# A hybrid decoder layer: rotary angles computed at the start, row scalings on ScalarE, five PSUM banks for the input projection, gate columns as stationary weights

## The chip, the cores and the metric

The kernel runs on one core of a Trainium2 chip. The metric is the device time of one execution in microseconds (us), taken as the median of several runs. Beside it stands one profiled execution, from which all rows below are read.

## What is computed

One decoder layer over 256 tokens of width 2048, in float32. Two projections of the conditioning vector `c` and of the normalised tokens feed two causal mixers, whose outputs share one output projection; then comes an expert channel mixer (PEER) over 16384 experts.

```python
mod = jax.nn.silu(c) @ w_ada + b_ada                    # 6 x 2048 shifts, scales, gates
h = modulate(rms_norm(x, norm1_g), shift1, scale1)
proj = h @ w_in                                         # 2048 x 6160
gq, gk, gv, gg, ga, mq, mk, mv = jnp.split(proj, offs, axis=-1)
log_a = jax.nn.log_sigmoid(ga @ gla_w_a2 + gla_b_a) / 16    # ga: 16 columns a token
o_gla = gla_attention(...); o_gla = rms_norm(o_gla, gla_norm_g) * silu(gg)
qm, km = partial_rotary(rms_norm(mq, ...), positions), partial_rotary(rms_norm(mk, ...), positions)
o_moba = moba_attention(qm, km, mv)                     # softmax rows p = exp(s - max) / sum
x = x + gate1 * (jnp.concatenate([o_gla, o_moba]) @ w_out)
x = x + gate2 * peer_ffn(modulate(rms_norm(x, norm2_g), shift2, scale2), ...)
```

With 256 tokens there is one MoBA block, so that the attention is causal within it. The rotary part needs the cosine and sine of 16 angles for every token.

## The kernel before

The kernel has a **front** (normalisation, projections, mixers; here up to about 545 us) and, behind it, the PEER part. The change touches the front alone. There, TensorE (PE) computes `w_in` and `w_out` products with operands split into a high and a low float32r half (`mm3`: three matmuls for a product). A block of weights of 128 x 1024 (512 KB) is loaded by SP (`w_load`), ScalarE makes its high half (`split_hi`, L164) and GpSimd (POOL) its low half (`split_lo`, L168), both some three blocks ahead.

The work is a list `items` of **steps**, one weight block each: 96 of the input projection (`project`, 12 matmuls with 512 columns), then 32 of the output projection. A column block of the projection takes two PSUM banks, one for each half of the tokens, and spans one step in steps 0 to 23, two in steps 24 to 71 and four from 72 on. When it is through, `after(tt)` adds the bank to an SBUF tile on VectorE (DVE, L486) or, the first time, copies it on ScalarE (L484); that is issued one step later (`late`). Banks come from three pools: `mm_ps` has three banks, `tp_ps` two, `at_ps` two. The tag `acc` has one.

DVE has a second stream of work: the product of `silu(c)` with `w_ada`, 160 loads of 512 KB in the front (`ada_load`, `ada_op`). An operation multiplies one loaded block into an accumulator (L260, L262, L265; mostly two instructions of 512 columns). How many run in a step is decided when the program is built, by a planned time `clock["PE"]` that `pe` advances with each matmul's columns. Every load that is used up issues the next (SP waits for that buffer, and what stands behind it in SP's queue waits too). DVE runs in program order: sums of banks, ada operations, and the steps of generators (`begins`) that are moved on once a step.

Those generators are what is touched: `small_loads` (from step 2) loads the positions among others, converts them (L400) and forms angles on POOL (L405); `angle_steps` (from step 12) reduces the angles on DVE (L427 to L441), takes the sine (L443) and multiplies the tables `tabs` (L449); `attend` (from step 76) divides the softmax rows on DVE (L551, L552), `normed` (in `gla`) scales rows of the GLA output (L720). `first_h` makes a quarter of the modulated input `h1`; step 24 is the first that needs the second quarter (L189). The 16 gate columns `pga` are computed in four groups, at column block 7, with the tokens as stationary weights and 16 columns moving; `gla` then transposes them.

Of the kernel before, what the change touches and what calls it, by code (L numbers as in the profile page):

```python
# [46 lines left out]
GLA = 90  # L47
# [24 lines left out]
def hybrid_layer(ctx, tc, x, xt, c, pos, w_ada0, w_ada, w_gate, b_cols, n1g, w_in, w_ga, wa2, ba, gla_g, q_g, k_g,  # L72
# [320 lines left out]
    ga = c1.tile([128, 2, 16], F32, name="ga")  # L393

    def small_loads():
        D_ = nc.sync
# [4 lines left out]
        V.tensor_tensor(gahl[:, 1], wga, gahl[:, 0].bitcast(F32), op=OP.subtract)
        D_.dma_start(out=wa2t[0:16], in_=wa2)
        D_.dma_start(out=wa2t[16:17], in_=ba)
        for tt in range(2):
# [10 lines left out]
    cs = c1.tile([128, 2, 2, 16], F32, name="cs")  # L415
    tabs = c1.tile([128, 2, 2, 4, 16], F32, name="tabs")
    freq = c1.tile([128, 16], F32, name="freq")
    fr = np.power(np.float32(500000.0), -np.arange(16, dtype=np.float32) * np.float32(2.0 / 32))
    for i in range(16):
        G.memset(freq[:, i:i + 1], float(fr[i]))  # L420
    posf = c1.tile([128, 2], F32, name="posf")
    ang = c1.tile([128, 2, 2, 16], F32, name="ang")
    kk = c1.tile([128, 2, 2, 16], F32, name="kk")
    magic = 1.5 * 2.0 ** 23

    def reduce_by(a, k, period, bits, n):
        V.tensor_scalar(k, a, 1.0 / period, magic, op0=OP.mult, op1=OP.add)  # L427
        V.tensor_scalar(k, k, magic, None, op0=OP.subtract)
        for p in _pieces(period, bits, n):
            V.scalar_tensor_tensor(a, k, -p, a, op0=OP.mult, op1=OP.add)  # L430

    def angle_steps():
        reduce_by(ang[:, :, 1], kk[:, :, 1], 2 * math.pi * 4096, 7, 4)
        yield
        reduce_by(ang[:, :, 1], kk[:, :, 1], 2 * math.pi, 10, 3)
        yield
        V.tensor_scalar(ang[:, :, 0], ang[:, :, 1], math.pi / 2, None, op0=OP.add)
        yield
        reduce_by(ang[:, :, 0], kk[:, :, 0], 2 * math.pi, 10, 3)
        yield  # L440
        V.tensor_scalar(ang, ang, 3.1415925, -3.1415925, op0=OP.min, op1=OP.max)  # L441
        yield
# [13 lines left out]

    def project(q, n, hf, group, part):

        first, last = (q, hf) == group[0], (q, hf) == group[-1]
        if first:  # L460
            held["ps"] = [mm_ps(), mm_ps()]
# [10 lines left out]
        if n == 7:  # L472
            pga = mm_ps("pga")
            rows = [(q_, k) for q_, hf_ in group for k in range(2 * hf_, 2 * hf_ + 2)]
            for tt in range(2):
                for q_, k in rows:
                    ts, cs_ = slice(128 * tt, 128 * (tt + 1)), slice(16 * (4 * q_ + k), 16 * (4 * q_ + k + 1))
                    mm3(pga[:, 16 * tt:16 * (tt + 1)], h1[q_][:, 0, k, ts], h1[q_][:, 1, k, ts], gahl[:, 0, cs_], gahl[:, 1, cs_],
                        (q_, k) == rows[0], (q_, k) == rows[-1])

        def after(tt):
# [5 lines left out]
            if tt and pga is not None:  # L487
                p3 = pga[:, 0:32].rearrange("p (t r) -> p t r", t=2)
                if q == 0 and hf == 0:
                    V.tensor_copy(ga, p3)  # L490
                else:
                    V.tensor_tensor(ga, ga, p3, op=OP.add)
# [38 lines left out]
    def attend(tt, h0):  # L531
# [20 lines left out]
        V.tensor_tensor(sm, sm, den[:, :, None].to_broadcast([128, nh, 128 * nk]), op=OP.mult)  # L552
# [35 lines left out]
    def gla():  # L588
        pgT = tp_ps("pgT")
        for tt in range(2):  # L590
            P.transpose(pgT[0:16, 128 * tt:128 * (tt + 1)], ga[:, tt], ident)
        yield
        V.tensor_copy(gaT[0:16], pgT[0:16, 0:T])
        yield
# [117 lines left out]
        def normed(tt, oo, sq):  # L712
# [7 lines left out]
            V.tensor_tensor(oo, oo, r[:, :, None].to_broadcast([128, 8, 128]), op=OP.mult)  # L720
# [95 lines left out]
    for step, it in enumerate(items):  # L816
# [592 lines left out]
```

## Time and profile before

| | us |
|---|---|
| median of three runs (2169.94 to 2176.66) | 2176.55 |
| the profiled execution, its own time | 2170.98 |
| its span, first to last instruction | 2169.2 |
| PE busy in the span | 2058.6 (95%) |
| DVE busy | 1626.8 (75%) |
| POOL / ACT busy | 937.5 / 891.2 |
| moved by DMA | 484.10 MB, 223 GB/s |

The page gives shares over the whole span; the stages have different limits, so the reading starts from the front's stretches. A row of the timeline shows the start, the duration from first to last instruction of a group, and in brackets the idle time before it with the instruction that ended it. "PEclk" is the granted clock of PE: 1.00 is 2.4 GHz and 0.50 is 1.2 GHz.

### The profile page before, as it was taken

The page shows a single profiled execution, that of the slowest core. Times are in us where ns is not written, and L with a number is a line of the kernel's source. Part 1 is how long each engine was busy: PE and PEld are TensorE (multiplying, and loading weights), DVE is VectorE, ACT ScalarE, POOL GpSimd, SP SyncE. Part 2 cuts the span into 40 slices and gives each one's busy share as a digit, 9 for nine tenths or more (in the row PEclk, how much of TensorE's full clock was granted, in tenths as well). Part 3 has the DMA queues.
Part 4 walks back from the last instruction along what each step waited for, and adds up shares of the span by engine and source line. Part 5 has one row for each costly group of instructions (what it writes and reads, how often), then busy time and mean ns, then how long its engine had stood idle before and what let it go on. Part 6 is the DMA issues. An engine that isn't in the chain of part 4 may idle for free.

```text
span 2169.2 us, 33001 instructions
## 1 busy us (share of the span) xinstructions
PE 2058.6 (95%) x12470; PEld 1795.2 (83%) x12470; DVE 1626.8 (75%) x2784; ACT 891.2 (41%) x1184; POOL 937.5 (43%) x551
## 2 busy tenths in 40 slices
PE   4899989989898798999999999999999999999998
PEld 3677777889898798888888888888888888888886
DVE  6787888985785687878788776777677676777687
ACT  5433454533444233434334434444344444444443
POOL 3677855555578777666666666520000000000000
PEclk9899989999899899999999999999999999999999
DMA  8788978878764566667676777776666666666674
GB/s 300 284 298 310 349 271 310 301 270 316 217 214 150 127 166 155 178 183 192 181 211 182 190 203 191 210 207 215 217 223 219 211 224 210 226 220 220 200 238 142
DMA packets 201569, 484.10 MB, mean 223 GB/s; under 512 B 54833, under 2 KB 88113, under 8 KB 200770
## 3 DMA queue, kind: packets, MB, share of 16 engines
q1 hardware_dynamic: 163250, 476.59, 65.1%
q0 software_dynamic: 36864, 0.15, 4.7%
q10 hardware_dynamic: 1296, 5.24, 0.7%
q8 instruction: 99, 1.62, 0.3%
q14 instruction: 60, 0.49, 0.1%
HBM read 469.05 MB, written 12.85 MB: 222 GB/s over the span
## 4 chain that ended last, share of the span: by engine, by line
PE 72%; DVE 5%; POOL 2%; issue 1%; DMA 1%; ACT 0%; SPq 0%; DVEq 0%; ACTq 0%; POOLq 0%
PE out L134 24%; PE A L134 17%; PE pa L134 15%; PE rot L134 8%; PE mm L134 2%; PE pq L134 2%; PE pg L1179 1%; POOL hl L168 1%; DVE acc L262 1%; POOL eq L999 1%; PE po L134 1%; DMA raw<-in_w_ada_dram 0%; DVE hl L168 0%; PE ada_ps L134 0%; DMA spread<-zeros 0%
## 5 line engine op out<-in xcount | busy, mean ns | idle before, releaser
L164 ACT ACTIVATE hl<-raw 128x1024 fp32r<-128x1024 f32 x672 | 675.4, 1051 | 431.7 <-PE mm L134 148.3
L168 DVE TENSOR_TENSOR hl<-raw,hl 128x1024 fp32r<-128x1024 f32 x506 | 607.5, 1228 | 128.1 <-ACT hl L164 127.0
L1193 POOL DMA_INDIRECT spread<-worth,place x256 | 470.9, 1839 | 245.2 <-DMA spread<-worth,place 205.8
L134 PE MATMUL out<-hl,wt 128*128 128x512 f32 x2304 | 570.4, 390 | 0.0
L134 PEld LDWEIGHTS out<-hl,wt 128*128 128x128 f32 x2304 | 430.8, 188 | 89.8
L168 POOL TENSOR_TENSOR hl<-raw,hl 128x1024 fp32r<-128x1024 f32 x166 | 401.3, 2422 | 208.8 <-ACT hl L164 194.3
L134 PE MATMUL A<-hT,hl 128*128 128x512 f32 (+1 forms) x2144 | 389.3, 340 | 0.0
L134 PE MATMUL pa<-hT,hl 128*128 128x256 f32 x2928 | 372.3, 287 | 16.2 <-POOL hl L168 16.2
L134 PEld LDWEIGHTS A<-hT,hl 128*128 128x128 f32 x2144 | 333.1, 188 | 51.9
L134 PEld LDWEIGHTS pa<-hT,hl 128*128 128x128 f32 x2928 | 360.8, 194 | 17.6 <-POOL hl L168 17.4
L1337 POOL TENSOR_TENSOR fin<-fin,back 128x512 f32<-128x512 f32 x4 | 5.1, 1276 | 726.1 <-DVE fin L1336 726.1
L134 PE MATMUL mm<-hl,hT 128*128 128x512 f32 x1152 | 289.8, 409 | 29.0 <-DVE mq L486 4.0
L134 PEld LDWEIGHTS mm<-hl,hT 128*128 128x128 f32 x1152 | 222.2, 196 | 83.1 <-DVE mk L486 4.9
L262 DVE SCALAR_TENSOR_TENSOR acc<-raw,sc,acc 128x512 f32<-128x512 f32 (+1 forms) x308 | 217.1, 705 | 35.2 <-DMA raw<-in_w_ada_dram 27.7
L1329 DVE TENSOR_TENSOR accs<-accs,rot 128x512 f32<-128x512 f32 x252 | 171.7, 681 | 81.3 <-PE rot L134 81.1
L134 PE MATMUL rot<-hl,wt 128*128 128x512 f32 x768 | 219.2, 394 | 2.2 <-DVE mod L160 1.4
L134 PEld LDWEIGHTS rot<-hl,wt 128*128 128x128 f32 x768 | 141.0, 188 | 31.3 <-issue 3.5
L1050 ACT ACTIVATE gel<-both 128x256 f32<-128x256 f32 x67 | 28.1, 419 | 320.1 <-DVE both L1049 308.9
L1048 DVE COPY both<-A 128x256 f32<-128x256 f32 x67 | 28.4, 424 | 132.4 <-PE A L134 132.4
L1233 ACT ACTIVATE wt<-wf 128x256 fp32r<-128x256 f32 x128 | 53.5, 418 | 170.1 <-DVE wf L1229 119.3
L134 PE MATMUL pq<-hT,hl 128*128 128x256 f32 x768 | 100.1, 291 | 7.8 <-DVE hT L876 4.1
L1026 ACT ACTIVATE gel<-pa 128x256 f32<-128x256 f32 x61 | 23.4, 383 | 198.9 <-PE pa L134 180.0
(250 smaller groups left out, 1506.4 us busy)
## 6 DMA issues: line engine op xcount, KB each, us to landing
raw<-in_u_dram SPq DMA_DIRECT2D x256, 512.0 KB
raw<-in_v_dram SPq DMA_DIRECT2D x256, 512.0 KB
raw<-in_w_ada_dram SPq DMA_DIRECT2D x160, 512.0 KB
raw<-in_w_in_dram SPq DMA_DIRECT2D x96, 512.0 KB
raw<-in_w_out_dram SPq DMA_DIRECT2D x32, 512.0 KB
raw<-in_w_q_dram SPq DMA_DIRECT2D x32, 512.0 KB
raw<-in_w_gate_dram SPq DMA_DIRECT2D x32, 512.0 KB
spread<-zeros SPq DMA_DIRECT2D x26, 320.0 KB
```

The lines of the kernel that those rows point to most:

```text
L134: P.matmul(out, lhs, rhs, **kw)
L164: S.activation(t[:, 0], r, AF.Copy)
L168: eng.tensor_tensor(t[:, 1], r, t[:, 0].bitcast(F32), op=OP.subtract)
L262: V.scalar_tensor_tensor(acc, part, sc[:, kb:kb + 1], acc, op0=OP.mult, op1=OP.add)
L999: G.tensor_tensor(eq, eq, indf[:, tt, cc, :, None, :].to_broadcast([128, 2, 16, 16]), op=OP.mult)
L1026: S.activation(gel_of(j), pa[:, 0:T], AF.Gelu)
L1048: V.tensor_copy(both, pa[:, 0:T])
L1050: S.activation(gel_of(j), both, AF.Gelu)
L1179: P.matmul(pg[:, t].rearrange("p s j -> p (s j)"), p1[t // 8][:, t % 8 // 2, :, t % 2], p2[:, t // 2, :, :, t % 2].rearrange("p s j -> p ( ...
L1193: G.indirect_dma_start(flat, bass.IndirectOffsetOnAxis(ap=place[:, tt, k:k + 1], axis=0), worth[:, tt, k:k + 1], None, compute_op=OP.add)
L1233: S.activation(wt[:, 0], wf, AF.Copy)
L1329: V.tensor_tensor(acc[n, tt], acc[n, tt], ps, op=OP.add)
```

## The change

It has six parts.

- The load of the positions is issued second in SP's queue, and the rotary angles are computed right behind DVE's first constants, before its first ada operation; the products of positions and frequencies move from POOL to DVE. The generator that is left (`table_steps`) takes the sine and multiplies `tabs` on POOL instead of DVE.
- The division of the softmax rows, and the scaling of the GLA rows by their inverse norm, become one ScalarE instruction for each head (16 and 16 in all) with the factor as its scale.
- `in_ps` gives the input projection banks in turn from `mm_ps` (three) and `at_ps` (two), until step 73; then from `mm_ps` alone, as before.
- The gate columns `pga` are computed with the 16 columns of weights standing and 256 tokens moving, 48 matmuls in place of 96; the result is already transposed, so that two transposes and a copy in `gla` go, and DVE's copy or sum has 16 x 256 elements in place of 128 x 32.
- No more than two ada operations run from the planner in one step.
- The GLA generator starts at step 92 in place of 90 (it has two stages less).

```diff
+    nc.sync.dma_start(out=posi, in_=pos)
...
+    V.tensor_copy(posf, posi)
+    for tt in range(2):
+        V.tensor_scalar(ang[:, tt, 1], freq, posf[:, tt:tt + 1], None, op0=OP.mult)
+    reduce_by(ang[:, :, 1], kk[:, :, 1], 2 * math.pi * 4096, 7, 4)
+    reduce_by(ang[:, :, 1], kk[:, :, 1], 2 * math.pi, 10, 3)
+    V.tensor_scalar(ang[:, :, 0], ang[:, :, 1], math.pi / 2, None, op0=OP.add)
+    reduce_by(ang[:, :, 0], kk[:, :, 0], 2 * math.pi, 10, 3)
+    V.tensor_scalar(ang, ang, 3.1415925, -3.1415925, op0=OP.min, op1=OP.max)
...
-                V.tensor_tensor(tabs[:, i, :, j], cs[:, :, c_], qkg[:, i:i + 1, 16 * g_:16 * (g_ + 1)].to_broadcast([128, 2, 16]), op=OP.mult)
+                G.tensor_tensor(tabs[:, i, :, j], cs[:, :, c_], qkg[:, i:i + 1, 16 * g_:16 * (g_ + 1)].to_broadcast([128, 2, 16]), op=OP.mult)
...
+    def in_ps(name="mm"):
+
+        held["turn"] = held.get("turn", -1) + 1
+        return (mm_ps if held["turn"] % 5 < 3 or ada["step"] >= ATTENDS[0] - 3 else at_ps)(name)
...
-            held["ps"] = [mm_ps(), mm_ps()]
+            held["ps"] = [in_ps(), in_ps()]
...
-            for tt in range(2):
-                for q_, k in rows:
-                    ts, cs_ = slice(128 * tt, 128 * (tt + 1)), slice(16 * (4 * q_ + k), 16 * (4 * q_ + k + 1))
-                    mm3(pga[:, 16 * tt:16 * (tt + 1)], h1[q_][:, 0, k, ts], h1[q_][:, 1, k, ts], gahl[:, 0, cs_], gahl[:, 1, cs_],
-                        (q_, k) == rows[0], (q_, k) == rows[-1])
+            for q_, k in rows:
+                cs_ = slice(16 * (4 * q_ + k), 16 * (4 * q_ + k + 1))
+                mm3(pga[0:16, 0:T], gahl[:, 0, cs_], gahl[:, 1, cs_], h1[q_][:, 0, k], h1[q_][:, 1, k],
+                    (q_, k) == rows[0], (q_, k) == rows[-1])
...
-        V.tensor_tensor(sm, sm, den[:, :, None].to_broadcast([128, nh, 128 * nk]), op=OP.mult)
+        for h in range(nh):
+            S.activation(sm[:, h], sm[:, h], AF.Copy, scale=den[:, h:h + 1])
...
-            V.tensor_tensor(oo, oo, r[:, :, None].to_broadcast([128, 8, 128]), op=OP.mult)
+            for h in range(8):
+                S.activation(oo[:, h], oo[:, h], AF.Copy, scale=r[:, h:h + 1])
...
-        while coming and 1.456 * (len(raws) + ada["loaded"]) + LEAD < clock["PE"] + (SLOPE * step + MORE * max(0, step - 58)) / 100:
+        most = ada["done"] + 2
+        while coming and ada["done"] < most and 1.456 * (len(raws) + ada["loaded"]) + LEAD < clock["PE"] + (SLOPE * step + MORE * max(0, step - 58)) / 100:
```

Three places show how instructions move. On DVE, at the start of the program (constants, then the ada accumulator `acc`), the order before was:

```order
L325 MEMSET chunk_of 128x2
L326 MEMSET chunk_of 64x1
L327 MEMSET chunk_of 64x1
L260 TENSOR_SCALAR acc<-raw,sc 128x256
L262 SCALAR_TENSOR_TENSOR acc<-raw,sc,acc 128x256 x7
```

and now it is, from the same memset on (the first nine instructions of the angles are left out here):

```order
L343 TENSOR_SCALAR kk<-ang 128x2x16
L344 TENSOR_SCALAR kk<-kk 128x2x16
L346 SCALAR_TENSOR_TENSOR ang<-kk,ang 128x2x16 x3
L353 TENSOR_SCALAR ang<-ang 128x2x16
L343 TENSOR_SCALAR kk<-ang 128x2x16
L344 TENSOR_SCALAR kk<-kk 128x2x16
L346 SCALAR_TENSOR_TENSOR ang<-kk,ang 128x2x16 x3
L355 TENSOR_SCALAR ang<-ang 128x64
L261 TENSOR_SCALAR acc<-raw,sc 128x256
L263 SCALAR_TENSOR_TENSOR acc<-raw,sc,acc 128x256 x7
```

All of the angles stand ahead of the first ada operation. On DVE around steps 11 to 14, where sums of the banks into `mq` begin, the order before was:

```order
L265 SCALAR_TENSOR_TENSOR total<-raw,sc,acc 128x512
L427 TENSOR_SCALAR kk<-ang 128x2x16
L428 TENSOR_SCALAR kk<-kk 128x2x16
L430 SCALAR_TENSOR_TENSOR ang<-kk,ang 128x2x16 x4
L486 TENSOR_TENSOR mq<-mq,mm 128x512 x2
L260 TENSOR_SCALAR acc<-raw,sc 128x512
L262 SCALAR_TENSOR_TENSOR acc<-raw,sc,acc 128x512
L427 TENSOR_SCALAR kk<-ang 128x2x16
L428 TENSOR_SCALAR kk<-kk 128x2x16
L430 SCALAR_TENSOR_TENSOR ang<-kk,ang 128x2x16 x3
L486 TENSOR_TENSOR mq<-mq,mm 128x512
```

and now it is:

```order
L266 SCALAR_TENSOR_TENSOR total<-raw,sc,acc 128x512
L484 TENSOR_TENSOR mq<-mq,mm 128x512 x2
L261 TENSOR_SCALAR acc<-raw,sc 128x512
L263 SCALAR_TENSOR_TENSOR acc<-raw,sc,acc 128x512
L441 MEMSET qkcol 32x2
L484 TENSOR_TENSOR mq<-mq,mm 128x512
```

The angle steps that stood ahead of each pair of sums are gone. On PE at the third group of gate columns (steps 36 to 39), before and now:

```order
L134 MATMUL mm<-hl,hT 128x512 x108
L134 MATMUL pga<-gahl,hT 128x16 x24
L134 MATMUL ada_ps<-ones,total 128x1 x4
L134 MATMUL mm<-hl,hT 128x512 x108
L134 MATMUL ada_ps<-ones,total 128x1 x4
```

```order
L134 MATMUL mm<-hl,hT 128x512 x96
L134 MATMUL ada_ps<-ones,total 128x1 x4
L134 MATMUL mm<-hl,hT 128x512 x12
L134 MATMUL pga<-hT,gahl 16x256 x12
L134 MATMUL mm<-hl,hT 128x512 x84
L134 MATMUL ada_ps<-ones,total 128x1 x4
```

The 24 narrow matmuls become 12 with 256 columns, and the ada column that ended behind them now ends a step earlier.

## Rows read from the trace of the kernel before

**Rows 1.** windows: stretch and us, busy by engine, PEclk, DMA share, GB/s

```profile
40.00:57.30 17.30, 16.14 (x80) 12.36 (x78) 9.72 (x21) 12.09 (x19) 8.18 (x4) 1.00 0.97 345
57.30:130.80 73.50, 61.55 (x258) 49.04 (x258) 61.69 (x103) 28.71 (x37) 49.17 (x23) 0.91 0.75 272
130.80:231.40 100.60, 96.94 (x438) 80.17 (x439) 74.42 (x108) 33.86 (x32) 76.56 (x32) 0.97 0.88 322
231.40:338.00 106.60, 98.85 (x470) 82.82 (x469) 88.62 (x136) 54.61 (x96) 73.29 (x36) 0.94 0.81 295
338.00:545.00 207.00, 190.82 (x1368) 171.14 (x1367) 161.95 (x254) 83.85 (x122) 112.06 (x50) 0.96 0.86 304
545.00:2169.00 1624.00, 1581.31 (x9820) 1389.49 (x9819) 1202.77 (x2100) 660.67 (x857) 608.01 (x379) 0.99 0.67 197
```

**Rows 2.** timeline, PE: start, us, form; in brackets idle before and who ended it

```profile
69.93 14.01 PE L134 MATMUL mm<-hl,hT 128*128 128x512 f32 x54 [2.25 <-ACT gqk L484]
...
87.32 2.93 PE L134 MATMUL mm<-hl,hT 128*128 128x512 f32 x6 [3.38 <-DVE mq L486]
...
101.11 12.67 PE L134 MATMUL mm<-hl,hT 128*128 128x512 f32 x42 [3.16 <-DVE mk L486]
...
130.83 18.89 PE L134 MATMUL mm<-hl,hT 128*128 128x512 f32 x82 [1.56 <-DVE hT L189]
...
195.07 14.15 PE L134 MATMUL mm<-hl,hT 128*128 128x512 f32 x54 [2.45 <-DVE gv L486]
...
277.80 2.89 PE L134 MATMUL mm<-hl,hT 128*128 128x512 f32 x6 [3.90 <-DVE mv L486]
...
475.05 1.94 PE L725 MATMUL tp<-ident,oo 128*128 128x128 f32 x8 [4.76 <-DVE oo L720]
```

**Rows 3.** timeline, DVE: the wait for positions

```profile
57.33 0.17 DVE L400 CAST posf<-posi 128x2 f32<-128x2 int32 x1 [4.29 <-DMA posi<-in_pos_dram]
```

**Rows 4.** groups by line, DVE, 57.3 to 130.8 us: count, busy, mean ns

```profile
L430 DVE SCALAR_TENSOR_TENSOR ang<-kk,ang 128x32 f32<-128x32 f32 x10 | 6.0, 597 | 0.3
...
L427 DVE TENSOR_SCALAR kk<-ang 128x32 f32<-128x32 f32 x3 | 3.2, 1083 | 0.0
...
L449 DVE TENSOR_TENSOR tabs<-cs,qkg 128x32 f32<-128x32 f32 x8 | 2.4, 354 | 0.0
```

**Rows 5.** timeline, DVE: first ada operation; two sums a pair of steps apart

```profile
7.88 0.49 DVE L260 TENSOR_SCALAR acc<-raw,sc 128x256 f32<-128x256 f32 x1 [3.99 <-DMA raw<-in_w_ada_dram]
...
141.59 0.69 DVE L486 TENSOR_TENSOR mq<-mq,mm 128x512 f32<-128x512 f32 x1 [0.68 <-PE mm L134]
...
147.03 0.69 DVE L486 TENSOR_TENSOR mk<-mk,mm 128x512 f32<-128x512 f32 x1 [0.63 <-PE mm L134]
```

**Rows 6.** timeline, PE, gate columns; then group, 256 columns moving (480:500)

```profile
174.99 2.74 PE L134 MATMUL pga<-gahl,hT 128*128 128x16 f32 x24
...
315.17 6.90 PE L134 MATMUL pga<-gahl,hT 128*128 128x16 f32 x48
...
L134 PE MATMUL mm<-mixg,hl 128*128 128x256 f32 x150 | 19.1, 285 | 0.0
```

**Rows 7.** tiles ang, sm, oo: ns min/median/max of DVE's operations

```profile
L430 DVE SCALAR_TENSOR_TENSOR ang<-kk,ang x10: 191/192/2215, 83.8 to 100.3; 128x32 f32<-128x32 f32 x10
...
L552 DVE TENSOR_TENSOR sm<-sm,den x6: 691/1309/2662, 314.7 to 367.5; 128x512 f32<-128x512 f32 x6
...
L720 DVE TENSOR_TENSOR oo<-oo,rs x2: 1218/2284/3349, 460.4 to 471.6; 128x1024 f32<-128x1024 f32 x2
```

**Rows 8.** timeline, ACT, DVE, POOL: eight scalings, an exponential's end, reciprocals, rstd

```profile
302.69 2.45 ACT L513 ACTIVATE qn<-mk,rs 128x128 f32<-128x128 f32 x8 [2.62 <-POOL rs L127]
...
333.67 0.19 ACT L549 ACTIVATION_READ_ACCUMULATOR sm<-sm,mx 128x1 f32 x1
...
337.78 0.15 DVE L551 RECIPROCAL den<-den 128x2 f32<-128x2 f32 x1
...
469.88 1.64 POOL L127 TENSOR_TENSOR rs<-rs,nhalf 128x8 f32<-128x8 f32 x1
```

More of the change, by code (lines that the diff above doesn't have):

```diff
@@ L46 @@
 ATTENDS = (76, 79, 79, 83, 85, 86)
-GLA = 90
+GLA = 92
 SILU = 98
@@ L327, in hybrid_layer, with reduce_by @@
     V.memset(chunk_of[64:128, 1:2], 0.0625)
+    cs = c1.tile([128, 2, 2, 16], F32, name="cs")
+    tabs = c1.tile([128, 2, 2, 4, 16], F32, name="tabs")
+    freq = c1.tile([128, 16], F32, name="freq")
+    fr = np.power(np.float32(500000.0), -np.arange(16, dtype=np.float32) * np.float32(2.0 / 32))
+    for i in range(16):
+        G.memset(freq[:, i:i + 1], float(fr[i]))
+    posf = c1.tile([128, 2], F32, name="posf")
+    ang = c1.tile([128, 2, 2, 16], F32, name="ang")
+    kk = c1.tile([128, 2, 2, 16], F32, name="kk")
+    magic = 1.5 * 2.0 ** 23
+    def reduce_by(a, k, period, bits, n):
+        V.tensor_scalar(k, a, 1.0 / period, magic, op0=OP.mult, op1=OP.add)
+        V.tensor_scalar(k, k, magic, None, op0=OP.subtract)
+        for p in _pieces(period, bits, n):
+            V.scalar_tensor_tensor(a, k, -p, a, op0=OP.mult, op1=OP.add)
+    V.tensor_copy(posf, posi)
[6 more added lines that the diff above has]
+    V.tensor_scalar(ang, ang, 3.1415925, -3.1415925, op0=OP.min, op1=OP.max)
     ss = [wk.tile([128, 2], F32, name="ssh") for _ in range(2)]
@@ L412, in small_loads, with table_steps @@
         D_.dma_start(out=ncol[:, 1], in_=n2g)
[L415 to L442, printed above, removed]
+    def table_steps():
         S.activation(cs, ang, AF.Sin)
@@ L472, in project @@
         if n == 7:
-            pga = mm_ps("pga")
+            pga = in_ps("pga")
             rows = [(q_, k) for q_, hf_ in group for k in range(2 * hf_, 2 * hf_ + 2)]
-            for tt in range(2):
-                for q_, k in rows:
-                    ts, cs_ = slice(128 * tt, 128 * (tt + 1)), slice(16 * (4 * q_ + k), 16 * (4 * q_ + k + 1))
-                    mm3(pga[:, 16 * tt:16 * (tt + 1)], h1[q_][:, 0, k, ts], h1[q_][:, 1, k, ts], gahl[:, 0, cs_], gahl[:, 1, cs_],
-                        (q_, k) == rows[0], (q_, k) == rows[-1])
+            for q_, k in rows:
+                cs_ = slice(16 * (4 * q_ + k), 16 * (4 * q_ + k + 1))
+                mm3(pga[0:16, 0:T], gahl[:, 0, cs_], gahl[:, 1, cs_], h1[q_][:, 0, k], h1[q_][:, 1, k],
+                    (q_, k) == rows[0], (q_, k) == rows[-1])
         def after(tt):
@@ L487, in after @@
             if tt and pga is not None:
[L488 removed]
                 if q == 0 and hf == 0:
[L490 removed]
+                    V.tensor_copy(gaT[0:16], pga[0:16, 0:T])
                 else:
[L492 removed]
+                    V.tensor_tensor(gaT[0:16], gaT[0:16], pga[0:16, 0:T], op=OP.add)
         return (lambda: after(0)), (lambda: after(1))
@@ L588, in gla @@
     def gla():
[L589 to L594, printed above, removed]
         ges, gTT = [big("ge", 0), None], big("gTT", 1)
@@ L806, in squares @@
             pe(sums2[tt][:, 0:1], sq[:, 128 * tt:128 * (tt + 1)], ones[:, 0:1], start=fb == 0, stop=fb == KB - 1)
-    begins = [(SMALL, small_loads()), (ANGLES, angle_steps()), (1, turn_x(range(EARLYX, 8))), (GLA, gla()), (SILU, gate_silu()), (RESID, residual())]
+    begins = [(SMALL, small_loads()), (ANGLES, table_steps()), (1, turn_x(range(EARLYX, 8))), (GLA, gla()), (SILU, gate_silu()), (RESID, residual())]
     begins += zip(FIRSTS, (first_h(0, 2, 2), first_h(1), first_h(2), first_h(3)))
```

5 lines of the change are left out of this document (removed).

## The prediction

> **What bounds the kernel now.** I read first the windows that cut the span into stretches, then PE's timeline inside the front for its gaps, then DVE's timeline and groups at those gaps, and last the single operations that the change moves. Behind 545 us PE is busy 1581 of 1624 us at a clock of 0.99 [rows 1], and nothing there is edited: what the front saves should arrive at the end undiminished, so I look for all of it in the front.
>
> In the front PE is the engine with most work in every stretch, but it loses time in two ways, and both are in [rows 1]: idle time (stretch less busy) and granted clock (1 less PEclk, times the stretch). From 57.3 to 130.8 us (A) that is 11.95 idle and 6.6 of clock; from 130.8 to 231.4 (B) 3.7 and 3.0; from 231.4 to 338 (C) 7.75 and 6.4; from 338 to 545 (D) 16.2 and 8.3. Together some 64 us: a ceiling that no edit here can pass by waits alone. The long gaps end on DVE [rows 2]: a bank that DVE has not yet added up (3.38, 3.16, 2.45, 3.90 us), the second quarter of the input (1.56), the scaled GLA rows (4.76). So DVE's order of work sets PE's pace, with DVE busy 61.7 of 73.5 us in A, and SP's loads hang on DVE too: in A they move 272 GB/s, while the stretch just before reached 345 [rows 1].
>
> **The sum, part by part,** against the profiled execution's 2170.98 us (span 2169.2, 1.8 around it). The median of the runs shown is 5.6 us above that execution; I keep to the profiled one.
>
> **Angles, stretch A.** Removed from DVE are a wait of 4.29 us for the positions, in a busy DMA queue [rows 3], and the angle steps and tables, 6.0 + 3.2 + 2.4 = 11.6 us in three groups [rows 4]. Queued behind that wait were ada operations, whose buffers SP needed before it could issue the next weight block: the 2.25 us gap at 69.9, which ends on a ScalarE copy, is its echo [rows 2]. The angle steps stand directly ahead of the late sums, as the second place of the order shows. With them gone A is bounded by three floors: PE's own 61.55 less 6.6 of lost clock, 55.0 us; DVE's 61.7 - 11.6, 50.1; the loads, 272 x 73.5 = 20.0 MB, at the 345 GB/s of the stretch before, 57.9. The highest leaves a gain of 15.6 of the 73.5. Three engines near their floors take turns in waiting, so I take 60.5, a gain of **13.0**; lowest 3 (the echo and little else), highest 15.6.
>
> What takes the steps over: about 21 small instructions ahead of DVE's first ada operation. One that meets no POOL traffic takes 0.19 us [rows 7], so some 4.0 us, and DVE waits there 3.99 us for its first weights [rows 5]. They hide, just; if that cover were gone they would cost up to their 4 us. The new load in front of SP's queue shifts all others by one issue, which I set at **0.5** lost (bounds 0 and 4). The tables cost POOL eight small products; no row shows one on POOL, so between DVE's smallest and largest form of such a step, 0.19 and 2.2 us [rows 7], 1.5 to 18 us; I take the low end, since POOL idles 24 of A's 73.5 us, and that idle time hides it; at the high end POOL's low halves would be late and take most of A's gain.
>
> **Five banks, stretches B and C.** A pair of steps takes 147.03 - 141.59 = 5.44 us of PE time [rows 5], 2.72 a step. With three banks PE stops when a sum is late by half a column block's time; two more banks let it go one whole block further, 2.72 us up to step 23 and 5.44 from 24 to 71. The gaps of 2.45 and 3.90 us [rows 2] are inside that and vanish until step 73; those from then on stay, and so do waits that are not for a bank. I take 2.45 in B and 4.5 of the 7.75 in C, and of the lost clock two thirds in B (2.0 of 3.0) and two fifths in C (2.5 of 6.4), which I put down to these gaps and the narrow matmuls below. A bank more costs nothing by itself: `at_ps` is idle until step 76.
>
> **Gate columns.** The group at 174.99 us takes 2.74 us, that at 315.17 6.90 [rows 6], part of it at half clock. A matmul with 256 columns moving takes 19.1 / 150 = 0.127 us [rows 6], so 12 and 24 of them take 1.5 and 3.05: gains of **1.2** (B) and **3.85** (C). It could be less if 16 standing columns cost more than 128, for which no row speaks; bound 0. The planner counts 48 x 256 columns for these in place of 96 x 16, 4.5 us of its clock, and so draws about three ada operations forward; the cap of two in a step spreads them. Both shift DVE's work earlier without adding any; nothing counted.
>
> B then gains 1.2 + 2.45 + 2.0 = **5.65** (bounds 0, and 3.7 + 3.0 + 1.2 = 7.9), C 3.85 + 4.5 + 2.5 = **10.85** (bounds 0, and 7.75 + 6.4 + 3.85 = 18).
>
> **Row scalings, stretch D.** DVE's softmax division has a median of 1.31 us and reaches 2.66, its smallest being 0.69; the GLA scaling took 1.22 and 3.35 [rows 7]. On ScalarE eight scalings take 2.45 us [rows 8]. At 475 us PE waits for the second GLA scaling. ScalarE can begin when POOL's inverse norm is there, 469.88 + 1.64 = 471.5, and half of the heads, enough for the first transposes, are done 1.2 us later, at 472.7 in place of 475.05: **2.3**. DVE loses 6 x 1.3 + 2 x 2.3 = 12.4 us of work in a stretch in which PE idles 16.2; I take **3.0** of that, and **1.0** of clock. D gains 6.3. Its bounds: a loss of 5.7, if ScalarE's 1.23 us for four and 2.45 for eight heads lay wholly on the path in place of DVE's smallest 0.69 and 1.22; a gain of 12.4, if all of DVE's work did.
>
> The Trainium skill speaks against this part: ScalarE: Activation LUTs, Rules for kernel authors, puts multiplications on VectorE, and the page's time for an ACTIVATE would make a softmax division on ScalarE dearer than 0.69 us. By that rule D would lose some 3.5 us where I count 5.3 won, and the sum would be near 2152. In this kernel the rows decide: the median on DVE is twice its smallest, beside a busy POOL, and DVE's is the queue that PE waits for.
>
> **The sum**: 13.0 + 5.65 + 10.85 + 6.3 = 35.8 gained, 0.5 lost. Some comes back: in 470 us in place of 505 the front's loads (302 GB/s on average over the five stretches) must run at 325, near the 345 of the best one, and DVE waits for loads in order, with the sums behind it. I take a fifth of the gain, 7.5. 2170.98 - 35.8 + 0.5 + 7.5 = **2143 us**.
>
> **The rivals.**
> - *All of it arrives* (0.12): nothing comes back, A is at its floor, and C's idle time goes whole: 7.5 + 2.6 + 3.3 + 1.5 more, 2128. For it: the gaps in [rows 2] are each shorter than what covers them now. Against: the loads' floor in A.
> - *The waits move to the loads* (0.19): DVE, freed, waits for ada loads. A gains half (6.5), the gate columns 5.05, the GLA rows 2.3: 2157.
> - *No change* (0.15): the loads' issue stays tied to DVE's and POOL's order and the front keeps its 302 GB/s, so that only about 3 us of PE time goes: 2168. Against it: the low 272 GB/s of A has a cause that is removed.
> - *ScalarE becomes the bound, slower* (0.08): its scalings wait for DVE's reciprocal, in order, and behind them stands the high half of the next weight block. At 333.86 us an exponential ended, at 337.78 its reciprocal began [rows 8], 3.9 us later. The point is the 5.4 us that two blocks in hand last: if the reciprocal comes later than that, PE loses a step, 2.7 us, and about half as much in clock (A: 6.6 beside 11.95), 4.2 at each of six attention groups and two norms, 34 in all, and D's 6.3: 2143 + 34 + 6.3 = 2183. Against it: ScalarE is busy 84 of 207 us in D, and DVE gets lighter.
>
> **How the numbers follow.** About 0.3% (6.5 us) is what a measurement of this kernel can tell from no change. The forecast has 0.46, its own range being 2130 to 2156; with it the first two rivals are faster by more than that, 0.77. The third is within, 0.15; the fourth slower, 0.08. The range 2120 to 2172 takes in the first three rivals and the bounds of the terms save their sums, and leaves out the slower case and the tails, some 0.15.
>
> **What would show it.** In the changed profile step 24 should begin near 118 us in place of 130.8 (if it is above 125, the angles were not what held A); DVE's first ada operation should begin below 8.9 us; the five gaps of [rows 2] that end on a bank, 15.1 us together, should fall below 5; the gate columns should take 0.13 us each; the transposes of the second GLA half should wait below 3 us. The prediction fails if DVE's waits for ada loads grow by more than 15 us, or if PE waits for weight blocks after step 76.

## The result, and the profile after

The changed kernel takes 2149.82 us (median of 4 runs, 2147.24 to 2152.65) where the kernel before, on the same chip, takes 2173.24 (4 runs, 2166.93 to 2176.66): a ratio of 0.9898, 95% interval 0.9873 to 0.9923. By the ratio that is 22 us gained; 28 were forecast.

The windows of the changed kernel, cut at about the same places of the work as [rows 1] from A on (columns as there):

```profile
57.30:117.30 60.00, 54.33 (x243) 43.68 (x242) 46.80 (x74) 28.12 (x35) 47.85 (x28) 0.97 0.92 336
117.30:215.00 97.70, 96.87 (x447) 80.23 (x448) 77.25 (x114) 36.99 (x35) 80.55 (x34) 1.00 0.93 346
215.00:312.00 97.00, 90.25 (x437) 74.11 (x435) 88.67 (x129) 51.96 (x96) 69.64 (x34) 0.96 0.85 315
312.00:524.00 212.00, 196.53 (x1357) 175.16 (x1358) 152.66 (x247) 94.27 (x151) 112.68 (x50) 0.93 0.84 294
524.00:2148.00 1624.00, 1581.58 (x9817) 1389.84 (x9815) 1203.00 (x2097) 661.58 (x857) 607.36 (x379) 0.99 0.66 197
```

The last stretch is 1624 us in both, with PE busy 1581 in both: all that was won was won in the front. A fell from 73.5 to 60.0 us, with loads at 336 GB/s in place of 272. B and C fell from 207.2 to 194.7. D rose from 207.0 to 212.0, at a clock of 0.93 in place of 0.96. So the places to look at are PE's gaps. The timeline of PE in the changed kernel, as [rows 2]:

```profile
74.20 2.17 PE L134 MATMUL mm<-hl,hT 128*128 128x512 f32 x8 [1.92 <-ACT gv L482]
78.14 6.90 PE L134 MATMUL mm<-hl,hT 128*128 128x512 f32 x22 [1.78 <-DVE hT L189]
...
117.36 18.90 PE L134 MATMUL mm<-hl,hT 128*128 128x512 f32 x82 [2.03 <-DVE hT L189]
...
262.72 1.07 PE L524 MATMUL tp<-ident,qn 128*128 128x128 f32 x8 [1.97 <-DVE qn L517]
277.49 1.90 PE L524 MATMUL tp<-ident,qn 128*128 128x128 f32 x8 [3.90 <-DVE qn L517]
...
404.27 1.09 PE L134 MATMUL pup<-gv,ge 64*64 64x128 f32 x16
410.12 1.84 PE L134 MATMUL ada_ps<-ones,total 128*128 128x1 f32 x8 [4.75 <-DVE states L679]
411.82 5.47 PE L134 MATMUL mm<-mixm,hl 128*128 128x256 f32 x24
417.22 0.55 PE L134 MATMUL po<-states,gTT 64*64 64x128 f32 x4
```

The five gaps of [rows 2] that end on a bank, 15.1 us together, are gone; one of 1.92 us that ends on ScalarE's copy is left, and from step 73 on, where the five banks end, two that end on DVE's sums (0.85 and 2.03 us). New ones stand in their place: 1.97 and 3.90 us for the rotated heads (`qn`, L517), and 4.75 us for the GLA's running states at 410. Behind the last, 24 matmuls with 256 columns take 5.47 us, while 24 such take 3.14 elsewhere in D (at 395.92 us, for one). From the third state update (`pup`, 404.27) to the first read (`po`, 417.22) the changed kernel needs 12.95 us. In the kernel before the same two stand 4.08 us apart:

```profile
427.84 1.09 PE L134 MATMUL pup<-gv,ge 64*64 64x128 f32 x16
428.86 3.13 PE L134 MATMUL mm<-mixm,hl 128*128 128x256 f32 x24
431.92 0.44 PE L134 MATMUL po<-states,gTT 64*64 64x128 f32 x4
```

That is 8.87 us more. What stands there differs by one row, the mod sums `ada_ps` (PE sums a finished column of the `w_ada` product over the partitions, and DVE puts the result into `mod`). In the kernel before they stand further on and take 0.95 us by themselves, at 438.10, so some 8 of the 8.87 us are lost. The order of PE's instructions around it, before and after, with nothing of time in it:

```
before:  pup x16 | mm x24 | po ... (16 groups) | ada_ps x8 | mm x24
changed: pup x16 | ada_ps x8 | mm x24 | po ...
```

DVE's timeline in the changed kernel shows what the states wait for (start, us, form):

```profile
403.00 1.13 DVE L679 SCALAR_TENSOR_TENSOR states<-states,dec,pup 128x128 f32<-128x128 f32 x4
404.02 0.50 DVE L783 SCALAR_TENSOR_TENSOR x2T<-mm,mod,x2T 128x256 f32<-128x256 f32 x1
404.42 3.14 DVE L263 SCALAR_TENSOR_TENSOR acc<-raw,sc,acc 128x512 f32<-128x512 f32 x4
...
408.25 0.72 DVE L664 COPY_PREDICATED ge<-allow,pa 128x512 f32<-128x512 uint32 x1
408.86 1.11 DVE L679 SCALAR_TENSOR_TENSOR states<-states,dec,pup 128x128 f32<-128x128 f32 x4
```

The mod sums take a bank of the two that the state updates use; the second update leaves its bank at 410.0, behind an ada operation of 3.14 us. The theory I took from this: angles, banks and gate columns gain as forecast, and the planner (the planned time that decides how many ada operations run in a step), which now counts 4.5 us more of PE time for the gate columns, draws ada operations forward and so moves the mod sums to a place where they stop PE. The rivals: what A gains comes back as lateness of DVE in C and D whatever the order; the scalings cost on ScalarE what they save on DVE.

### The profile page after: what moved, and what is told of

Read it like the earlier page. It is cut to its first block, busy times and chain, and to the rows that moved or that the text cites. A ratio compares the mean times of both kernels' runs of the same rounds, so it can differ in the third digit from the quotient of the medians.

```text
span 2148.2 us, 32945 instructions
## 1 busy us (share of the span) xinstructions
PE 2049.0 (95%) x12420; PEld 1786.5 (83%) x12420; DVE 1612.2 (75%) x2769; ACT 902.9 (42%) x1216; POOL 939.9 (44%) x557
## 4 chain that ended last, share of the span: by engine, by line
PE 80%; DVE 11%; DMA 3%; POOL 3%; issue 2%; ACT 0%; DVEq 0%; SPq 0%; POOLq 0%; ACTq 0%
PE out L134 24%; PE A L134 18%; PE pa L134 16%; PE mm L134 10%; PE rot L134 8%; DMA raw<-in_w_ada_dram 3%; DVE acc L263 3%; PE pq L134 1%; POOL hl L168 1%; PE pg L1173 1%; POOL eq L993 1%; PE ada_ps L134 1%; DVE rt L514 1%; PE po L134 1%; DVE hl L168 1%
## 5 line engine op out<-in xcount | busy, mean ns | idle before, releaser
L134 PEld LDWEIGHTS pa<-hT,hl 128*128 128x128 f32 x2928 | 361.1, 194 | 17.5 <-POOL hl L168 17.4
L134 PE MATMUL mm<-hl,hT 128*128 128x512 f32 x1152 | 281.0, 402 | 12.1 <-DVE hT L189 3.8
L263 DVE SCALAR_TENSOR_TENSOR acc<-raw,sc,acc 128x512 f32<-128x512 f32 (+1 forms) x308 | 217.3, 705 | 31.0 <-DMA raw<-in_w_ada_dram 23.2
```

Of the source, the lines that this page charges most:

```text
L134: P.matmul(out, lhs, rhs, **kw)
L263: V.scalar_tensor_tensor(acc, part, sc[:, kb:kb + 1], acc, op0=OP.mult, op1=OP.add)
```

## The experiments

All are variants of the changed kernel. Ratios are to the kernel before, run on the same chip; a difference of two ratios times 2171 us (before) is given in us with the interval that follows from both.

| run | us, median | ratio, 95% interval | against the changed kernel, us |
|---|---|---|---|
| e1_late_angles | 2161.31 | 0.9962 (0.9947 to 0.9976) | +13.9 ± 6 |
| e2_three_banks | 2154.68 | 0.9926 (0.9908 to 0.9945) | +6.1 ± 7 |
| e3_narrow_gate | 2146.95 | 0.9898 (0.9884 to 0.9912) | 0.0 ± 6 |
| e4_dve_scaling | 2148.85 | 0.9907 (0.989 to 0.9924) | +2.0 ± 7 |
| e5_pace | 2135.98 | 0.9848 (0.9824 to 0.9872) | -10.9 ± 8 |
| e6_ada_bank | 2136.66 | 0.9846 (0.9823 to 0.9869) | -11.3 ± 7 |
| e7_wait_only | 2155.93 | 0.9939 (0.9917 to 0.9961) | +8.9 ± 7 |
| e8_no_cap | 2147.4 | 0.9893 (0.9871 to 0.9916) | -1.1 ± 7 |
| e9_early_rope | 2133.15 | 0.9818 (0.9783 to 0.9853) | -17.4 ± 9 |
| e10_pace_dve | 2144.98 | 0.9876 (0.9841 to 0.9911) | -4.8 ± 9 |
| e11_pace_bank | 2137.2 | 0.9826 (0.979 to 0.9863) | -15.6 ± 10 |
| e12_all | 2134.08 | 0.9827 (0.9791 to 0.9863) | -15.4 ± 10 |

The first four undo one part each. Their sum, 13.9 + 6.1 + 0.0 + 2.0 = 22.0, is the 22 us of the whole change. All four differences go back to the same four runs of the changed kernel, so that the sum is uncertain by some 20 us; that the parts do not overlap is not shown by it. One of them, the gate columns, costs nothing to undo (0.0 ± 6).

### Angles back in their place

```diff
-    nc.sync.dma_start(out=posi, in_=pos)
...
-    V.tensor_copy(posf, posi)
-    reduce_by(ang[:, :, 1], kk[:, :, 1], 2 * math.pi * 4096, 7, 4)
...
+    def angle_steps():
+        reduce_by(ang[:, :, 1], kk[:, :, 1], 2 * math.pi * 4096, 7, 4)
+        yield
...
-                G.tensor_tensor(tabs[:, i, :, j], ...)
+                V.tensor_tensor(tabs[:, i, :, j], ...)
```

> The changed kernel with one part undone: the positions' load, the angle steps and the tables stand again where they were, in the steps from 2 and 12 on, all on VectorE; the rest of the change stays. Theory (the prediction's term for A): step 24 begins near 130 us again instead of 117.4, and as nothing behind A gives it back, the time is 10 to 13.5 us above the changed kernel's, 2160 to 2163. Rival (what A gains waits later, at VectorE's rotary steps or the GLA's states): step 24 is as late as that, but the waits of 1.97, 3.90 and 4.75 us on VectorE shrink, and the time is only 3 to 6 us above, 2153 to 2156.

Step 24 begins at 127.45 us, 10.1 us later than in the changed kernel, where about 13 were expected, and the time is 13.9 us up: the theory holds. Nothing behind A gives the gain back: the wait for the states is 4.75 us here too, and the profiled executions, 10.1 us apart at step 24, are 9.2 apart at their ends. The groups of DVE show why the steps were dear. First this run, 57 to 127.4 us, then the changed kernel, 4 to 9 us (count, busy us, mean ns, idle before):

```profile
L430 DVE SCALAR_TENSOR_TENSOR ang<-kk,ang 128x32 f32<-128x32 f32 x10 | 6.1, 608 | 0.3
L449 DVE TENSOR_TENSOR tabs<-cs,qkg 128x32 f32<-128x32 f32 x8 | 3.1, 453 | 0.0
L428 DVE TENSOR_SCALAR kk<-kk 128x32 f32<-128x32 f32 x3 | 2.7, 885 | 0.1
L427 DVE TENSOR_SCALAR kk<-ang 128x32 f32<-128x32 f32 x3 | 2.0, 679 | 0.0
```

```profile
L346 DVE SCALAR_TENSOR_TENSOR ang<-kk,ang 128x32 f32<-128x32 f32 x10 | 1.9, 192 | 0.3
L344 DVE TENSOR_SCALAR kk<-kk 128x32 f32<-128x32 f32 x3 | 0.5, 182 | 0.1
L343 DVE TENSOR_SCALAR kk<-ang 128x32 f32<-128x32 f32 x3 | 0.5, 181 | 0.1
```

The same instructions cost 10.8 us where POOL makes its low halves of weights, and 2.9 us at the start, where POOL is busy 0.00 of the 4.6 us. Of the 24 steps of the four groups 17 took 0.18 to 0.19 us; the other seven, 0.49 to 2.35 us long, lie within POOL's subtractions for all but 0.05 us of their time. One of them, DVE's row and POOL's:

```profile
79.49 2.29 DVE L428 TENSOR_SCALAR kk<-kk 128x32 f32<-128x32 f32 x1
76.58 5.16 POOL L168 TENSOR_TENSOR hl<-raw,hl 128x1024 fp32r<-128x1024 f32 x2
```

The Trainium skill (SBUF — State Buffer, Who interferes with whom) says that VectorE's operations with two SBUF inputs, or in its two-port modes, share a port pair with GpSimd; these rows agree, with 0.18 us against means up to 0.89.

### Only the wait for the positions gone

```diff
+    nc.sync.dma_start(out=posi, in_=pos)
...
+    posf = c1.tile([128, 2], F32, name="posf")
+    V.tensor_copy(posf, posi)
     ss = [wk.tile([128, 2], F32, name="ssh") for _ in range(2)]
...
     def small_loads():
-        D_.dma_start(out=posi, in_=pos)
...
-        V.tensor_copy(posf, posi)
```

The diff is against the run before this one; the load stands at the front of SP's queue again, as in the change.

> The changed kernel with the angle steps and the tables back in their old place on VectorE, but with the positions loaded and converted at the start as in the change, so that only the wait of 4.29 us for them is gone. Undoing the whole part cost 13.5 us. Theory (the prediction: the wait with what is queued behind it is the smaller half, the 11.6 us of work in front of the late sums the larger): step 24 begins near 122 to 125 us, and the time is 5 to 9 us above the changed kernel's. Rival (the wait and its echo in the weight loads are nearly all): step 24 near 118, and the time within 3 us of the changed kernel's.

Step 24 begins at 126.42 us, later than the 122 to 125 expected, and the time is 8.9 us above the changed kernel's. The work ahead of the late sums is the larger part, as forecast; the wait is worth 1 us of step 24, less than forecast, and 5 ± 6 of the time. Gaps in A that end on DVE's sums are back, as in the kernel before, if not the one for `mq`:

```profile
97.42 8.62 PE L134 MATMUL mm<-hl,hT 128*128 128x512 f32 x30 [2.88 <-DVE mk L490]
108.04 3.00 PE L134 MATMUL mm<-hl,hT 128*128 128x512 f32 x12 [1.30 <-DVE gqk L490]
113.46 1.05 PE L134 MATMUL ada_ps<-ones,total 128*128 128x1 f32 x8 [2.42 <-DVE total L266]
126.42 3.92 PE L134 MATMUL mm<-hl,hT 128*128 128x512 f32 x16 [1.58 <-DVE hT L189]
```

### Three banks

```diff
-        return (mm_ps if held["turn"] % 5 < 3 or ada["step"] >= ATTENDS[0] - 3 else at_ps)(name)
+        return mm_ps(name)
```

> The changed kernel with one part undone: three banks for the input sums instead of five. Theory (the prediction's terms for banks): the gaps of 2 to 4 us that end on a bank come back in B and C, with some lost clock, and the time is 7 to 11 us above the changed kernel's, 2157 to 2161. Rival (the banks only move the waits to the rotary steps, 5.9 us in C): the gaps return, the waits for the rotated heads fall by about as much, and the time is 2 to 5 us above, 2152 to 2155.

The time is 6.1 us up, between the two theories, and the interval takes in both ends; the profiled executions differ by 3.5 us, which speaks for the rival. PE's waits from 117 to 330 us (total, times, longest) tell more, first here, then in the changed kernel:

```profile
...
PE mm L134 <- DVE gv L484: 2.4, 1, 2.4
PE mm L134 <- DVE mk L484: 2.0, 2, 1.3
PE mm L134 <- DVE mv L484: 2.0, 2, 1.3
PE mm L134 <- DVE gqk L484: 1.6, 2, 1.1
PE mm L134 <- DVE mq L484: 1.6, 1, 1.6
```

```profile
PE tp L524 <- DVE qn L517: 5.9, 2, 3.9
...
```

With three banks 9.6 us of waits for sums come back, and the 5.9 us for rotated heads go. So the banks let PE run on until it meets the next thing that DVE owes it, here the rotary groups; what is left of them in waits is the difference, 3.7 us.

### Narrow gate columns, and the planner's count

```diff
-                mm3(pga[0:16, 0:T], gahl[:, 0, cs_], gahl[:, 1, cs_], h1[q_][:, 0, k], h1[q_][:, 1, k], ...)
+                    mm3(pga[:, 16 * tt:16 * (tt + 1)], h1[q_][:, 0, k, ts], h1[q_][:, 1, k, ts], gahl[:, 0, cs_], gahl[:, 1, cs_], ...)
...
```

> The changed kernel with one part undone: GLA's gate columns again as 48 and 96 narrow matmuls with the two transposes behind them, as before. Theory: these groups take 2.7 and about 6 to 7 us again in place of 1.5 and 2.95, and the time is 4 to 6 us above the changed kernel's, 2154 to 2156. Rival (the planner counts 4.5 us less of TensorE time, so ada operations come later and the wait of 4.75 us for the states at 410 us goes): the two cancel, and the time is within 2 us of the changed kernel's or below it.

The time is that of the changed kernel, 0.0 ± 6, which by itself does not shut out the theory's 4 to 6 us. The trace speaks for the rival: the wait at the states is gone, though the last gate group takes 6.78 us again in place of 2.95. (The GLA generator starts at step 90 again here, with its two transposes.) The next run tells the two apart: wide columns, counted as before; it is called the pace run below. Its edit is one line behind the gate columns' loop:

```diff
+            clock["PE"] -= 3 * len(rows) * (T - 2 * 16) / 1000 * 0.422
```

> The changed kernel with one line added: the planner's count of TensorE time takes the gate columns as it did before (16 columns a matmul), so that ada operations are drawn forward no more; the instructions are the same, only their order differs. In the changed kernel's order the last two mod sums before GLA's reads (ada_ps) stand directly behind the third state update and wait 4.75 us for a bank that the second update frees; here they stand some 16 groups later, behind the reads. Theory: that wait and its lost clock are what the narrow gate columns won back in their run; the wait goes, and the time is 5 to 8 us below the changed kernel's, 2142 to 2145. Rival (the narrow columns' run came out level for another reason, and VectorE only waits elsewhere in D): within 2 us of the changed kernel's.

It gains 10.9 us on the changed kernel, more than I gave it, though the interval takes in the 5 to 8. Third update and first read are 4.08 us apart again, with no gap:

```profile
397.20 1.09 PE L134 MATMUL pup<-gv,ge 64*64 64x128 f32 x16
...
401.28 0.43 PE L134 MATMUL po<-states,gTT 64*64 64x128 f32 x4
```

Step 24 begins at 113.35 us, too, against 117.36. Some 3 us of that stand already where PE goes on with the second half of the first input quarter (75.10 against 78.14 us): one ada operation that waits 5.37 us for its load stands ahead of that half's factors in the changed kernel, and behind them here. (In the profiles with the change's angles, banks and count, four of them, step 24 begins between 114.6 and 117.4; in the six with the old count between 110.8 and 114.1.) That lead is gone by the last gate group, 291.92 against 292.76 us: PE waits 2.23 and 4.38 us at the transposes of rotated heads on the way. (The first of these ends on `mod`: the heads were ready 1.2 us before, and DVE had yet to take the mod sums out of a bank.) From there to the third update the pace run's profiled execution is 6.2 us quicker, and without the changed kernel's wait of 2.45 us for softmax rows at 314.43; 8.87 us more come between update and read. Narrow against wide at the same count, the third run against this one, is 10.9 ± 6 us: the price of the gate columns when nothing hides it. The windows of both runs, the last gate group and the stretch behind it, show where most of it lies, first the narrow one:

```profile
294.20:301.05 6.85, 6.85 (x51) 6.81 (x50) 6.28 (x14) 2.60 (x9) 2.04 (x1) 0.78 0.68 233
301.05:358.90 57.85, 54.86 (x279) 45.99 (x279) 41.77 (x73) 30.97 (x67) 31.39 (x14) 0.94 0.87 328
```

```profile
291.90:294.87 2.97, 2.97 (x27) 2.44 (x26) 2.87 (x6) 2.19 (x9) 0.00 (x0) 1.00 0.50 193
294.87:349.40 54.53, 52.07 (x277) 42.99 (x274) 43.01 (x76) 31.27 (x68) 33.36 (x14) 1.00 0.94 348
```

The group itself is 3.9 us shorter, as forecast; the stretch behind it is another 3.3 us shorter, and the granted clock, 1.00 in place of 0.94 over 57.85 us, makes up as much. Together that is 7.2 of the 10.1 us by which the two profiled executions differ.

### Another bank for the mod sums, and no cap

```diff
-            mod_of(m, n, total, tp_ps("ada_ps"))
+            mod_of(m, n, total, (mm_ps if ada["step"] >= ATTENDS[0] else tp_ps)("ada_ps"))
```

> The changed kernel with one line changed: from the first attention step on, the mod sums (ada_ps) take one of the three banks of the projections in place of one of the two that the state updates also use. Order and pace stay. Theory: the wait of 4.75 us at 410 us is for the bank alone, and goes or falls below 1.5 us; time 4 to 8 us below the changed kernel's, 2142 to 2146. Rival (VectorE, late with the states, holds the reads as well): TensorE waits the same time one group later, at the output block or the reads, and the time is within 2 us.

11.3 us below the changed kernel, with its order and its count: the bank alone was the cause of the wait. Update and read are 4.98 us apart, the mod sums between them in 1.05 us, where the changed kernel needs 12.95. These 8.0 us are most of the 10.6 by which the two profiled executions differ:

```profile
403.48 1.09 PE L134 MATMUL pup<-gv,ge 64*64 64x128 f32 x16
404.50 1.05 PE L134 MATMUL ada_ps<-ones,total 128*128 128x1 f32 x8
...
408.46 0.44 PE L134 MATMUL po<-states,gTT 64*64 64x128 f32 x4
```

The fifth part, the cap, was taken out by itself (the sixth, the GLA generator's later start, was not):

```diff
-        most = ada["done"] + 2
-        while coming and ada["done"] < most and 1.456 * ... :
+        while coming and 1.456 * ... :
```

> The changed kernel without the cap of two ada operations in a step. Theory (the prediction: three operations stood in three of the steps before, so the cap moves next to nothing): within 2 us of the changed kernel's. Rival: runs of three operations, 9.4 us of VectorE in a row, hold up sums again, and the time is 3 to 5 us above.

No difference that can be seen, though -1.1 ± 7 does not shut out the rival's 3 to 5. DVE's ada operations stand elsewhere than in the changed kernel only around 300 and 430 us, and the wait for the states is 4.75 us here too. So the cap moves next to nothing. That is what this run's theory says; the prediction itself had said that the cap spreads what the count draws forward, and that does not hold.

### Scalings back on VectorE

```diff
-        for h in range(nh):
-            S.activation(sm[:, h], sm[:, h], AF.Copy, scale=den[:, h:h + 1])
+        V.tensor_tensor(sm, sm, den[:, :, None].to_broadcast([128, nh, 128 * nk]), op=OP.mult)
...
-            for h in range(8):
-                S.activation(oo[:, h], oo[:, h], AF.Copy, scale=r[:, h:h + 1])
+            V.tensor_tensor(oo, oo, r[:, :, None].to_broadcast([128, 8, 128]), op=OP.mult)
```

> The changed kernel with one part undone: both scalings, of the softmax rows and of GLA's normed rows, on VectorE again. Theory (the prediction's term for D): VectorE has 12 us more, the transposes of the second GLA half wait 4 to 5 us for it again, and the time is 3 to 6 us above the changed kernel's, 2153 to 2156. Rival (the rule that multiplications belong on VectorE): ScalarE's 1.2 us for four heads and 2.45 for eight were on the path, and the time is 2 to 5 us below, 2145 to 2148.

2.0 ± 7 us up: no verdict between them. At the place itself the wait for DVE is back, in size as the theory had it:

```profile
459.92 1.94 PE L716 MATMUL tp<-ident,oo 128*128 128x128 f32 x8 [4.01 <-DVE mod L160]
```

These transposes begin 42.6 us behind the first read, where the changed kernel's begin 39.7 us behind it. The thought was that in the changed kernel the wait for the states hides what the scalings are worth, so the same edit was made on the pace run.

> The pace run's kernel with both scalings (softmax rows, GLA's normed rows) on VectorE again: what ScalarE's share is worth where the wait for the states does not cover it. In the changed kernel, undoing it cost 2 us. Theory (the prediction's term, 6.3 us in D): 4 to 7 us above the pace run, a ratio of 0.9867 to 0.988, with the second GLA half's transposes waiting over 3.5 us for VectorE. Rival (VectorE's work there is covered by output blocks; only the one wait differs): 0 to 3 us above, and a last rival (multiplications belong on VectorE): below the pace run.

Its nearest kernel on the same chip is the run with pace and bank: 2144.98 (2140.97 to 2149.06) against 2137.2 (2128.13 to 2139.18), 7.8 us above without overlap; against the pace run, on another chip, 6 ± 9. The transposes of the second GLA half wait 4.97 us for DVE, as in [rows 2], where the pace run waits 1.73 for ScalarE, and begin 42.2 us behind the first read in place of 39.0:

```profile
447.99 1.94 PE L717 MATMUL tp<-ident,oo 128*128 128x128 f32 x8 [4.97 <-DVE oo L712]
```

That is 3.2 us (3.8 against the run with pace and bank), and 3.0 in the pair above: with and without the wait for the states the traces show nearly the same worth at this place, and that the wait hid any of it is not shown. What of the 7.8 us goes beyond that lies elsewhere; in the profiled executions, 3.5 us apart, this run is 1.9 us late already at the last gate group, ahead of the first scaling. Tiles of this run and of the changed kernel (ns min/median/max):

```profile
L550 DVE TENSOR_TENSOR sm<-sm,den x6: 691/1318/2410, 296.9 to 341.9; 128x512 f32<-128x512 f32 x6
L712 DVE TENSOR_TENSOR oo<-oo,rs x2: 1218/2170/3121, 433.0 to 444.7; 128x1024 f32<-128x1024 f32 x2
```

```profile
L550 ACT ACTIVATE sm<-sm,den x16: 385/448/512, 297.9 to 344.8; 128x128 f32<-128x128 f32 x8, 128x256 f32<-128x256 f32 x8
L713 ACT ACTIVATE oo<-oo,rs x16: 385/406/423, 441.6 to 458.5; 128x128 f32<-128x128 f32 x16
```

Of ScalarE's scalings of GLA's rows, the eight that met no POOL instruction took 0.41 to 0.42 us each, the eight beside a busy POOL 0.39 to 0.40. DVE's softmax division reaches three times its smallest: it took 0.69 us where no POOL instruction overlapped it, and 2.41 where one did for 2.23 us. The Trainium skill (ScalarE: Activation LUTs, Rules for kernel authors) says to use VectorE for a multiplication, not ScalarE. By that rule this run would lie below the pace run; it lies above it, by 6 ± 9 us, and above the run with pace and bank by ranges that do not overlap.

### Rotary groups one step earlier, and all together

```diff
-ROPES = (65, 66, 69, 73)
+ROPES = (64, 65, 68, 72)
...
         yield
+        yield
         d3 = dst.rearrange("p (h t) -> p h t", h=8)
```

> The changed kernel with the planner's old count of the gate columns (the pace run, ratio 0.985), and the four rotary groups started one step earlier, with one more empty step ahead of their transposes, which stay in their place. In the pace run TensorE waits 2.23 and 4.38 us for rotated heads. Theory (these waits are VectorE's order, as with the states): both fall below 1.5 us, and the time is 3 to 7 us below the pace run's, a ratio near 0.982 to 0.9835. Rival (VectorE is full there, 75 of 82 us, and only the sums become late instead): the waits move to the banks and the time is within 2 us.

> Pace and bank together: the planner's old count of the gate columns, and the mod sums in a projection's bank from the first attention step on. Theory (both cure one wait, that for the states): no more than either alone, a ratio of 0.983 to 0.986. Rival (two different gains): the sum of both, near 0.98.

> Pace, bank and the earlier rotary groups together, the version that should beat both kernels. Theory: as the run with pace and earlier rotary groups, a ratio of 0.980 to 0.984. Rival (the earlier groups only move VectorE's lateness): as pace and bank, 0.984 to 0.986.

These three ran on one chip, at 2133.15, 2137.2 and 2134.08 us, with ranges that overlap: what the earlier rotary groups or the second cure of the same wait add, 0 to 4 us, stays open, and so does the verdict between theory and rival in all three (the first is 6.5 ± 9 us below the pace run, which ran on another chip). In the first, the waits at the transposes of rotated heads (6.6 us in the pace run) fall to 1.4, and those for the mod sums rise from 3.3 to 6.7 (total, times, longest, 57 to 500 us):

```profile
PE ada_ps L134 <- DVE total L266: 6.7, 3, 3.3
...
PE tp L526 <- DVE mod L160: 1.4, 1, 1.4
```

Of the 5.2 us that went, 3.4 came back at other things that DVE owes. All three beat both kernels: 0.982 to 0.983 of the time before, with 0.986 the highest end of an interval.

## Why the prediction was right in direction and 7 us off in size, point by point

**Angles, 13.0.** Right in cause, and in size by the medians: step 24 came 13.5 us earlier, near the 118 forecast, and undoing the part costs 13.9 ± 6. In the traces undoing it moves step 24 by 10.1 us; what the other 3.4 of the 13.5 come from no run tells. The work of the steps was the larger half, the wait for the positions the smaller, but the wait was worth only 1 us of step 24. The steps' own cost at the start was nearly right: DVE's chain from 4.30 to 8.97 us is 4.7 us where 4.0 was forecast, and the first ada operation begins at 8.87 in place of 7.88 [rows 5]; no run tells that 1 us apart. POOL's eight products take 0.25 us each, the low end.

**Five banks, 6.95 in waits and part of 4.5 in clock.** The gaps went as said. Not all of it counted: the wait for `mv` in C [rows 2] turned into 5.9 us for the rotated heads, whose transposes stand in PE's order at a fixed step. 6.1 ± 7 came of it, 3.5 in the profiled executions.

**Gate columns, 5.05 and the other part of the clock.** The groups take 0.12 to 0.14 us a matmul (2.95 for 24, 0.86 for 6), as forecast; at one count the part, with the two transposes that go, is worth 10.9 ± 6, since the clock stays up behind it.

**The step that failed** is the sentence that the planner "draws about three ada operations forward" and that both this and the cap "shift DVE's work earlier without adding any; nothing counted". The work was no more, but its results came out earlier in PE's order as well: the mod sums moved ahead of the GLA's reads, into one of two banks that the state updates hold. Price: 8.0 us there by the trace of the run that changes the bank alone; in all 11.3 ± 7 by that run and 10.9 ± 8 by the run that undoes the count. Nor does the cap spread the operations. I had looked at the order where the change is and not at where the counted operations end.

**Scalings, 5.3 and 1.0 of clock.** The second GLA half went as forecast (its transposes wait 0.94 us in the changed kernel, where below 3 was forecast), and its worth at that place is 3.0 to 3.8 us in three pairs of traces, where 2.3 was forecast. The other 3.0 and the 1.0 of clock, from DVE's lighter load, stay open: the whole part is worth 2 ± 7 us in the changed kernel and 6 ± 9 or 7.8 without the wait for the states.

**What comes back, 7.5, to loads.** Wrong in cause, and near in size by luck. DVE's waits for ada loads fell from 27.7 to 23.2 us, so the rival that put the waits there is out, and the pace run, 11 us shorter, has more of them (30.5) and loses nothing by it. What came back is the 10.9 us of the planner's order. So, by the medians, 2143 missed by 7 us for three reasons that partly cancel: the planner's order cost 10.9 instead of 7.5, the banks and the scalings brought less, and the gate columns with their clock brought more. Each of these numbers is good to 6 to 8 us, so this account fits and is not shown term by term.

**The slower rival**, weight blocks behind ScalarE's scalings, is out: PE waits for no weight block in the front behind step 76. One softmax group shows its pattern in small, 2.45 us at 314.43 us, where the scalings stood behind DVE's reciprocal for 5.67 us. With the scalings on DVE PE waits 2.03 us at the same place, again for the reciprocal, so it is DVE's lateness and not ScalarE's work. The rivals at 2128 (whose last term, 1.5, has no row behind it) and at 2168 lie 18 us and more from the measured time; the one at 2157 is as near as the forecast, but its waits did not come.

## What to carry to other kernels

When an edit changes the numbers by which a planner orders work, read the order of every engine at the place where the moved work ends, not only where it begins, and ask which bank or buffer its last instruction takes and who holds it. A wait that is bought off runs on until the next thing that the late engine owes; price it by the difference of the two. Undoing one part at a time prices each part inside the whole, and a part that costs nothing to undo may hide a gain and a loss of the same size. Such prices share the error of the kernel they are taken from, so read the place in the two traces beside them.

## What the runs showed of the hardware

Behind the gap of 4.75 us PE ran at half clock for 7 us, and then at nearly full clock again (windows of the changed kernel, columns as in [rows 1]):

```profile
410.12:417.20 7.08, 7.08 (x32) 6.87 (x32) 4.51 (x10) 0.00 (x0) 0.00 (x0) 0.50 0.59 196
417.20:424.00 6.80, 6.80 (x54) 4.55 (x54) 3.46 (x5) 2.13 (x4) 2.35 (x1) 0.98 0.85 289
```

0.50 is 1.2 GHz of 2.4. The mod sums and the 24 matmuls behind them take 7.10 us here and 3.96 at full clock in the run that changes the bank, so that one wait cost its 4.75 us and 3.1 more. I had counted clock as a share of the idle time, about half; here it was two thirds. And the clock fell without any idle time in the narrow gate columns: PE is busy 6.85 of 6.85 us there, at a mean of 0.78, and the wide ones take their 2.97 us at 1.00.
